# Moving the middle blocks as two partition halves, block by block: a softmax-gradient kernel on one Trainium2 core

## The chip, the core and the metric

The kernel runs on one core of one Trainium2 chip. The metric is the device time of one execution in microseconds (us). Three runs of the kernel before gave 1248.84, 1248.91 and 1249.3 us; the median is 1248.91 us.

## What is computed

The input is a float32 array of 8 x 1024 rows with 8192 logits each, and one integer label for each row. The output is the gradient of the cross-entropy loss: the softmax of each row, with 1 subtracted at the label.

```python
logits_max = np.max(logits, axis=-1, keepdims=True)
exp_logits = np.exp(logits - logits_max)
softmax = exp_logits / np.sum(exp_logits, axis=-1, keepdims=True)
...
one_hot[batch_idx, seq_idx, labels] = 1.0
return (softmax - one_hot).astype(np.float32)
```

Input and output are 268.4 MB each, and each is moved once.

## The kernel before

**Tiles.** The 8192 rows are cut into 32 blocks of 256 rows. In a block each of the 128 partitions holds G = 2 neighbouring rows (t0 and t1), 32 KB each, which lie one behind the other in device memory. A block is therefore 8.39 MB, and one partition's share of it is one run of 64 KB. On-chip the tile X has SLOTS = 3 places for a block, so block b + 3 goes where block b was. All work on a row is done in place in X.

**Work on one row t** (each "row" is 128 partitions x 8192):
- `row_max` (L141): VectorE (DVE) takes the negated maximum, a tensor_reduce.
- `exponentials` (L149): ScalarE (ACT) writes exp(x - max) over the row and sums it.
- `mark` (L157): two short ACT operations prepare the one-hot row as bytes in PSUM (`hot`), two rows ahead. It has to wait until the row that used this half of `hot` is finished.
- `finish` (L169): DVE takes the reciprocal of the sum and then does x * r - hot in one scalar_tensor_tensor. For the last two rows this is done in two halves of the columns.

**Transfers.** Three strings, one letter for each of the 32 blocks, say how a block moves and in which order it is worked. `PIECES` (L88) gives the pieces of a letter: "r" is two transfers, one for each row, over all 128 partitions in runs of 32 KB; "s" is four, each one row over every other partition (0, 2, 4, ... or 1, 3, 5, ...); "w" is one transfer over all 128 partitions in runs of 64 KB.
- `load(b)` (L101) issues the loads of block b on the SP queue (the odd partitions of "s" on the ACT queue). A piece waits for those stores of block b - 3 that touch the same partitions and rows (`meets`, L94).
- `store(t)` (L114) is called behind the finish of each row and issues on the ACT queue those pieces whose last row is t, after a wait for that finish. The last two rows are stored in two column halves each, on SP and ACT.
- Before: loads are "s" for blocks 0 to 2, "r" for 3 and 4, "w" for 5 to 28 and "r" for 29 to 31. All stores are "r".

**Order.** It is written out by hand in the loop at L244. Engines take their instructions strictly in the order in which this loop issues them. With the letter "r" in `ORDER`, DVE works a row ahead: max(t1), finish(t0), max of the next block's t0, finish(t1). The next block's first maximum therefore stands on DVE ahead of the finish of this block's second row. The store of t0 is issued between, right behind finish(t0). With the letter "b" (L247) DVE does max(t0), max(t1), finish(t0), finish(t1) and turns to the next block only then. Loads of block b + 3 are put on SP at the end of turn b in both orders.

All these operations go through the helper `run` (L71), so the profile gives them all line L76; they are told apart by their tiles and shapes.

Of the kernel before, what the change touches and what calls it, by code (L numbers as in the profile page):

```python
# [7 lines left out]
P = 128  # L8
G = 2
SLOTS = 3  # L10

LOADS = "sssrrwwwwwwwwwwwwwwwwwwwwwwwwrrr"
STORES = "rrrrrrrrrrrrrrrrrrrrrrrrrrrrrrrr"
ORDER = "rrrrrrrrrrrrrrrrrrrrrrrrrrrrrrrr"


@with_exitstack
def kernel(
# [45 lines left out]
    with tc.tile_critical():  # L64
# [6 lines left out]
        def run(engine, waits, counter, method, **operands):  # L71

            waits = list(dict.fromkeys(waits))
            for w in waits[:-1]:
                engine.wait_ge(*w)  # L75
            instruction = getattr(engine, method)(**operands)  # L76
            for w in waits[-1:]:
                instruction._wait_ge(*w)
            step = 16 if method == "dma_start" else 1
            instruction.then_inc(counter, step)  # L80
            count[counter.name] = count.get(counter.name, 0) + step
            return counter, count[counter.name]

        every, rows = slice(0, P), slice(0, G)
        one = [slice(j, j + 1) for j in range(G)]
        halves = [slice(i, P, 2) for i in range(2)]
        sides = [slice(i * V // 2, (i + 1) * V // 2) for i in range(2)]
        PIECES = {  # L88
            "r": [(every, js) for js in one],
            "s": [(ps, js) for js in one for ps in halves],  # L90
            "w": [(every, rows)],
        }

        def meets(a, b):  # L94
            sets = [[set(range(*d.indices(n))) for d, n in zip(p, (P, G))] for p in (a, b)]
            return all(x & y for x, y in zip(*sets))
# [4 lines left out]
        def load(b):  # L101
            loaded[b] = []
            before = stored.get(b - SLOTS, [])
            for q, piece in enumerate(PIECES[LOADS[b]]):
                ps, js = piece
                free = [w for other, w in before if meets(piece, other)]
                queue = nc.scalar if LOADS[b] == "s" and ps == halves[1] else nc.sync
                w = run(
# [5 lines left out]
        def store(t):  # L114
            b, j = divmod(t, G)
            stored.setdefault(b, [])
            if t >= T - G:
# [6 lines left out]
                return  # L124
            for q, piece in enumerate(PIECES[STORES[b]]):
                ps, js = piece
# [30 lines left out]
        def mark(t):  # L157
            if t >= T:
                return
            w = run(  # L160
                nc.scalar, ([made] if t < G else [freed[t - G]]) + ([marked[t - 1]] if t else []), act, "activation",
                out=away[:], in_=count16[:], func=Act.Abs, bias=at(word, t), scale=1.0,
            )
            marked[t] = run(
                nc.scalar, [w], act, "activation",
                out=hot[:, t % G, :], in_=away[:], func=Act.Relu, bias=at(unit, t), scale=at(minus, t),
            )
# [76 lines left out]
        for b in range(B):  # L244
            t0, t1 = b * G, b * G + 1
            nxt = t1 + 1
            if ORDER[b] == "b":  # L247
                if t0 not in maxed:
# [20 lines left out]
            mark(t0 + G)  # L269
            ahead = nxt < T and ORDER[b + 1] == "r"  # L270
            if ahead:
# [41 lines left out]
```

## Time and profile before

| what | value |
|---|---|
| median of 3 runs | 1248.91 us |
| span of the profiled execution (first to last instruction) | 1246.6 us |
| DVE busy | 1120.2 us, 90% |
| ACT busy | 722.7 us, 58% |
| moved by DMA | 536.98 MB, mean 431 GB/s |

The page's span is the time that it gives for its execution; the median of the runs is 2.3 us longer. In the profile "DMA" in a table by slices is the mean busy share of the core's 16 DMA engines, in tenths where it is one digit. A "packet" is one contiguous run, so 32 or 64 KB here, and a few bytes for the signal that a transfer has landed. q1 is the queue that SP issues on, q10 that of ACT. "us to landing" counts from the issue of a transfer to its last byte.

### The profile page before, as it was taken

To read this page: it belongs to the slowest core of one execution; us is meant where nothing else is said; L and a number is where in the kernel's file an instruction comes from. 1 tells how busy PE (TensorE), PEld (TensorE's weight loads), DVE (VectorE), ACT (ScalarE), POOL (GpSimd) and SP (SyncE) were. 2 spreads that over 40 slices of the span, in tenths; PEclk is the share of its full clock that TensorE was granted. 3 is DMA by queue.
4 is the path that set the end of the run, shared out by engine and by line. 5 is a ranking of instruction groups with operands and counts; after the bars stand their busy time and mean duration, and the time that the engine had idled before them with its cause. 6 is when DMAs were issued, how large, how long until landed. Compare 5 with 4: busy or idle time off the path is not lost.

```text
span 1246.6 us, 809 instructions
## 1 busy us (share of the span) xinstructions
PE 0.4 (0%) x2; PEld 0.3 (0%) x2; DVE 1120.2 (90%) x208; ACT 722.7 (58%) x257; POOL 2.3 (0%) x7
## 2 busy tenths in 40 slices
PE   0000000000000000000000000000000000000000
PEld 0000000000000000000000000000000000000000
DVE  5999998889988889888898888998889988899995
ACT  2866664556555565465655655556556555566662
POOL 0000000000000000000000000000000000000000
DMA  9999999999999999999999999999999999999998
GB/s 406 413 431 434 437 432 444 435 437 421 433 429 437 443 423 433 434 431 435 430 441 435 422 435 435 434 440 426 432 434 431 433 446 434 422 430 435 429 434 383
DMA packets 15413, 536.98 MB, mean 431 GB/s; under 512 B 1808, under 2 KB 1808, under 8 KB 1840
## 3 DMA queue, kind: packets, MB, share of 16 engines
q10 hardware_dynamic: 9744, 276.89, 51.5%
q1 hardware_dynamic: 5664, 260.05, 48.3%
q14 instruction: 5, 0.04, 0.0%
HBM read 268.50 MB, written 268.44 MB: 431 GB/s over the span
## 4 chain that ended last, share of the span: by engine, by line
DMA 59%; DVE 26%; issue 11%; ACT 3%; DVEq 0%; ACTq 0%; SPq 0%
DMA X<-in_logits_dram 33%; DMA out_dram<-X 26%; DVE X L76 15%; DVE m L76 10%; ACT X L76 2%; DVEq L64 0%; DVE r L76 0%; ACT hot L76 0%; ACT away L76 0%; ACTq L76 0%; DVEq L75 0%; ACTq L308 0%; SPq L64 0%
## 5 line engine op out<-in xcount | busy, mean ns | idle before, releaser
L76 ACT ACTIVATE X<-X,m 128x8192 f32<-128x8192 f32 x64 | 455.8, 7122 | 365.2 <-DVE m L76 365.2
L76 DVE TENSOR_REDUCE m<-X 128x1 f32<-128x8192 f32 x64 | 555.6, 8682 | 105.4 <-DMA X<-in_logits_dram 105.4
L76 DVE SCALAR_TENSOR_TENSOR X<-X,r,hot 128x8192 f32<-128x8192 f32 (+1 forms) x66 | 560.1, 8489 | 3.8 <-ACT hot L76 1.6
L76 ACT ACTIVATE away<-count,word 128x2048 bf16<-128x2048 int16 x64 | 128.1, 2001 | 127.0 <-DVE X L76 127.0
L76 ACT ACTIVATE hot<-away,unit,minus 128x2048 int32<-128x2048 bf16 x64 | 131.9, 2061 | 2.1
L76 ACT ACTIVATION_READ_ACCUMULATOR X<-X,m 128x1 f32 x64 | 11.9, 186 | 0.0
L76 DVE RECIPROCAL r<-s 128x1 f32<-128x1 f32 x64 | 9.8, 153 | 0.0
L76 ACT ACT_TABLE_LOAD x1 | 1.3, 1283 | 5.3 <-issue 5.3
L76 DVE CAST lab_f<-lab_raw 32x256 f32<-32x256 int32 x1 | 0.5, 536 | 2.7 <-DMA lab_raw<-in_labels_dram 2.7
L76 POOL IOTA count<- 128x2048 int16 x1 | 1.8, 1823 | 0.0
L76 DVE TENSOR_TENSOR unit<-unit,part 128x64 f32<-128x64 f32 x3 | 0.7, 225 | 0.1
L76 DVE CAST lab<-hot 128x64 int32<-128x64 f32 x1 | 0.2, 224 | 0.5 <-PE hot L76 0.5
L76 DVE TENSOR_SCALAR part<-minus 128x64 f32<-128x64 f32 x3 | 0.6, 194 | 0.1
L76 PE MATMUL hot<-ident,lab_f 32*128 32x32 f32 x2 | 0.4, 298 | 3.3 <-DVE lab_f L76 3.3
L76 PEld LDWEIGHTS hot<-ident,lab_f 32*128 32x128 f32 x2 | 0.3, 192 | 3.3 <-DVE lab_f L76 3.3
L76 DVE CAST minus<-lab 128x64 f32<-128x64 int32 x1 | 0.2, 195 | 0.0
L76 DVE TENSOR_SCALAR word<-part 128x64 f32<-128x64 int32 x1 | 0.2, 195 | 0.0
L76 DVE TENSOR_SCALAR lab<-lab 128x64 int32<-128x64 int32 x1 | 0.2, 195 | 0.0
L76 DVE TENSOR_SCALAR unit<-minus 128x64 f32<-128x64 f32 x1 | 0.2, 195 | 0.0
L76 DVE TENSOR_SCALAR part<-lab 128x64 int32<-128x64 int32 x1 | 0.2, 194 | 0.0
L76 DVE TENSOR_SCALAR minus<-unit 128x64 f32<-128x64 f32 x1 | 0.2, 194 | 0.0
L76 POOL TENSOR_SCALAR_AFFINE_SELECT ident<-ident 32x32 f32<-32x32 f32 x1 | 0.2, 203 | 0.1
(5 smaller groups left out, 0.5 us busy)
## 6 DMA issues: line engine op xcount, KB each, us to landing
out_dram<-X ACTq DMA_DIRECT2D x62, 4096.0 KB, 30.4
X<-in_logits_dram SPq DMA_DIRECT2D x10, 4096.0 KB, 28.1
X<-in_logits_dram SPq DMA_DIRECT2D x6, 2048.0 KB, 32.6
X<-in_logits_dram ACTq DMA_DIRECT2D x6, 2048.0 KB, 37.1
out_dram<-X SPq DMA_DIRECT2D x2, 2048.0 KB, 12.7
out_dram<-X ACTq DMA_DIRECT2D x2, 2048.0 KB, 11.9
X<-in_logits_dram SPq DMA_DIRECT2D x24, 33.4
lab_raw<-in_labels_dram ACTq DMA_DIRECT2D x1, 64.0 KB, 1.8
```

The source lines that it names most:

```text
L76: instruction = getattr(engine, method)(**operands)
```

## The change

```diff
-LOADS = "sssrrwwwwwwwwwwwwwwwwwwwwwwwwrrr"
-STORES = "rrrrrrrrrrrrrrrrrrrrrrrrrrrrrrrr"
-ORDER = "rrrrrrrrrrrrrrrrrrrrrrrrrrrrrrrr"
+LOADS = "sssrrccccccccccccccccccccccccrrr"
+STORES = "rrccccccccccccccccccccccccrrrrrr"
+ORDER = "bbbbbbbbbbbbbbbbbbbbbbbbbbbbbbbb"
...
+        blocks_p = [slice(i * P // 2, (i + 1) * P // 2) for i in range(2)]
...
             "w": [(every, rows)],
+            "c": [(ps, rows) for ps in blocks_p],
```

The new letter "c" is two transfers, one for partitions 0 to 63 and one for partitions 64 to 127, each with both rows: 64 runs of 64 KB, 4.19 MB. Loads of blocks 5 to 28 are "c" where they were "w", and stores of blocks 2 to 25 are "c" where they were "r". As block b + 3 follows block b in its place, each lower half is loaded behind the store of the same lower half, and each upper half behind that of the upper. A "c" store covers both rows, so both of its transfers are issued behind finish(t1), where "r" issued the first behind finish(t0). All blocks are worked in the order "b". The first and last blocks move as before.

## The prediction

> **What bounds the kernel now.** I read the page's first lines, then DMA by stretches of time, then the chain that ended last. On the page:
>
> ```profile
> span 1246.6 us, 809 instructions
> PE 0.4 (0%) x2; PEld 0.3 (0%) x2; DVE 1120.2 (90%) x208; ACT 722.7 (58%) x257; POOL 2.3 (0%) x7
> DMA  9999999999999999999999999999999999999998
> DMA packets 15413, 536.98 MB, mean 431 GB/s; under 512 B 1808, under 2 KB 1808, under 8 KB 1840
> q10 hardware_dynamic: 9744, 276.89, 51.5%
> q1 hardware_dynamic: 5664, 260.05, 48.3%
> ```
>
> The two queues fill 99.8% of the time of 16 DMA engines: 0.998 x 1246.6 = 1244.1 us of work, and 2.5 us without. The table by stretches (us, engines, clock, DMA share, GB/s in the last column) says where:
>
> ```profile
> 2.00:44.00 42.00, 0.41 (x2) 0.28 (x2) 28.84 (x18) 20.71 (x8) 1.13 (x1) 1.00 1.00 426
> 44.00:166.00 122.00, 0.00 (x0) 0.00 (x0) 121.75 (x22) 81.77 (x30) 0.00 (x0) 1.00 1.00 430
> 166.00:1093.00 927.00, 0.00 (x0) 0.00 (x0) 829.86 (x144) 534.11 (x190) 0.00 (x0) 1.00 1.00 433
> 1093.00:1215.00 122.00, 0.00 (x0) 0.00 (x0) 121.75 (x21) 78.94 (x28) 0.00 (x0) 1.00 1.00 433
> 1215.00:1246.60 31.60, 0.00 (x0) 0.00 (x0) 18.02 (x7) 7.21 (x2) 0.00 (x0) 1.00 0.89 382
> ```
>
> DMA is full from 2 us to the tail, with the same 426 to 433 GB/s when only loads run (before 44 us) and when both directions do. DVE waits in the middle (830 of 927 us). So time is bytes over rate; an edit can gain only idle DMA, and there are 2.5 us of it.
>
> Per engine, q1 gives 0.483 x 16 x 1246.6 / 260.05 = 37.05 us per MB, q10 0.515 x 16 x 1246.6 / 276.89 = 37.10. That is 27 GB/s an engine, and 2.43 us for a run of 64 KB. q1 holds most of the 64 KB runs and q10 nearly all the 32 KB ones: the length of a run is worth 0.05 us per MB, under 1 us in all.
>
> How the engines share the work is seen in the middle of the trace, the DMA of 20 us in slices of 0.5 us (bytes are counted where a packet starts):
>
> ```profile
> DMA  9900193990009499300799960099300794960049
> GB/s 1704 393 0 0 66 852 131 918 1180 0 0 0 852 197 524 1442 131 0 0 328 721 393 1442 262 0 0 393 1573 131 0 0 328 655 197 1704 262 0 0 197 786
> q1 hardware_dynamic: 96, 6.29, 72.5%
> q10 hardware_dynamic: 95, 2.59, 30.0%
> ```
>
> Packets start in waves: peaks at slices 1, 9, 16, 23, 28 and 35, mostly 3.5 us apart, which is one 64 KB load (2.43 us) and one 32 KB store (1.21 us). All sixteen engines take a load together, then a store together, spread over about 0.75 us. This decides below.
>
> The chain repeats every two blocks:
>
> ```profile
> 482.00 26.58 DMA out_dram<-X
> 508.59 33.63 DMA X<-in_logits_dram
> 542.25 0.04 DVE m L76
> ...
> 551.04 8.76 DVE X L76
> 559.82 26.10 DMA out_dram<-X
> ```
>
> 77.8 us for two blocks, 38.9 each, is their 33.55 MB at 431 GB/s. The chain is stretched to the DMA rate; it does not set it.
>
> **The change part by part.**
>
> *Order "b" and the later store.* The DVE and ACT instructions are the same ones:
>
> ```profile
> L76 DVE TENSOR_REDUCE m<-X 128x1 f32<-128x8192 f32 x64 | 555.6, 8682 | 105.4 <-DMA X<-in_logits_dram 105.4
> L76 DVE SCALAR_TENSOR_TENSOR X<-X,r,hot 128x8192 f32<-128x8192 f32 x62 | 542.4, 8748 | 3.7 <-ACT hot L76 1.6
> L76 ACT ACTIVATE X<-X,m 128x8192 f32<-128x8192 f32 x64 | 455.8, 7122 | 365.2 <-DVE m L76 365.2
> ```
>
> A block costs DVE 2 x 8.68 + 2 x 8.75 + 2 x 0.15 (reciprocal) = 35.2 us in either order. In "b" the exponentials of t1 (7.1 us) end before finish(t0) (8.75 us) does, so finish(t1) waits for nothing. From the trace in order of time:
>
> ```profile
> 482.00 0.34 ACTq L76 DMA_DIRECT2D out_dram<-X  x1
> 499.44 0.34 ACTq L76 DMA_DIRECT2D out_dram<-X  x1
> 499.89 2.00 ACT L76 ACTIVATE away<-count,word 128x2048 bf16<-128x2048 int16 x1 [2.08 <-DVE X L76]
> 501.92 2.06 ACT L76 ACTIVATE hot<-away,unit,minus 128x2048 int32<-128x2048 bf16 x1
> 508.59 77.68 SPq L76 DMA_DIRECT2D X<-in_logits_dram  x3
> ```
>
> ACT now waits in one place for finish(t1) before it issues both store halves; behind it stand one mark and the next block's first exponentials, which need a maximum 8.7 us later anyway, and a mark takes 4.1 us (2.00 + 2.06). The first row's store, which now goes out 17.4 us ahead of the second's, waits for it.
>
> Does DMA run dry for it? With both queues equally served, a block's store takes 38.7 us (twice 8.39 MB at 433 GB/s); the lower half of block b + 3 loads behind the lower half of the store, the upper half needs 19.4 us more, then DVE 35.2: 93.3 us of the three periods (116.2 us) that a place in X has. 23 us are left, and two of the three places always hold a transfer. Cost 0. If that cover fails, DMA stands idle between a block's finish and its store's successors, priced with the rivals.
>
> *Transfers.* 24 loads become 48; stores stay at 66 issues. An issue takes 0.34 us on ACT; SP issues three in 77.7 us. More than 4,000 extra packets on q10 cost nothing visible above, so 24 x 16 more signals cost under 0.1 us. Cost 0.
>
> *64 KB stores, half the partitions.* Run length: between -1 us and 0. The partition range is what matters, and no transfer before stays within 64 neighbouring partitions. The bounds:
>
> ```profile
> X<-in_logits_dram SPq DMA_DIRECT2D x6, 2048.0 KB, 32.6
> X<-in_logits_dram ACTq DMA_DIRECT2D x6, 2048.0 KB, 37.1
> ```
>
> *Lower bound, nothing:* these "s" loads also have 64 partitions each, and they are all that moves until 44 us, at 426 GB/s. So 64 partitions as such are not slow. But they are every other one, spread over the whole memory.
>
> *Upper bound, twice the time:* at full rate each engine moves 27 GB/s with sixteenths of all the partitions, loads alone no faster than loads and stores. If the way into a group of partitions carries what one engine brings, sixteen engines inside one half have eight ways, two engines on each. Because they run in waves, the two meet: a packet takes 4.86 us instead of 2.43 less the offset between the two. Across a wave 0.75 us wide two engines are some 0.25 us apart, a tenth of a packet: factor 1.9, for loads and for stores, since each wave is of one direction. A lower half in flight beside an upper half does not help, for all engines serve one piece, then the other.
>
> The "s" row is nearest in size, the waves nearest in kind; no row decides. I take factor 1.9, and keep 1 and 2 for the range.
>
> The Trainium skill speaks against this change: its page "SBUF — State Buffer", section "Door 1: The DMA port swizzle", says that partitions 0 to 63 reach only the eight even ports of sixteen and 64 to 127 only the odd ones, at about 218 GB/s. Every other partition reaches all sixteen by that table, so the "s" rate agrees with it; no run here yet shows a contiguous half. By its figure the 402.65 MB of "c" would take an estimated 1847 us. The page "DMA: Bandwidth & Descriptors", section "Rules for kernel authors", says two transfers to disjoint partition halves "serialize".
>
> *Sum.* "c" carries 24 loads and 24 stores of 8.39 MB: 402.65 of 536.98 MB, 75.0%, so 932.9 of the 1244.1 us of DMA work; the rest is 311.2 us. 932.9 x 1.9 = 1772.5; with 311.2 and 2.5 idle the span is 2086 us. The runs' median is 2.3 us above the profiled span: **2089 us**. DVE's 35.2 us a block lie inside some 74 us of DMA.
>
> **The rivals.**
>
> *A, no change:* the halves run at full rate (each engine can reach any partition at 27 GB/s, or each half keeps to its own eight engines and both run side by side). For it: the "s" loads. No row speaks against it. DMA stays full, 1244.1 + 2.5 + 2.3 = 1249 us, 1247 to 1251; not slower. It decides if a 64 KB packet into a half still takes 2.43 us. By the page of the Trainium skill named above it would not.
>
> *B, half of it:* only one direction is limited, or the two engines of a way fall out of step and one loads while the other stores. Factor 1.5: 1399.4 + 311.2 + 4.8 = 1715 us. For it: an engine that takes its packet from the other queue first stays out of step. Against it: the waves are still sharp at 322 us.
>
> *C, four engines on one way:* if the 64 partitions are dealt so that sixteen engines first crowd into 32, factor up to 4: 3731.6 + 316.0 = 4048 us. Nothing in the rows excludes it.
>
> *D, DMA runs dry a little:* full rate, but in the tail the last block's 35.2 us of DVE come after its load, and if the backlog of stores has by then drained, up to half of that (17.6 us) is idle: 1249 to 1267. Against it: 20 us of queued stores and 8.4 MB of the block before (19.4 us) cover it.
>
> *E, faster:* at most 2.5 us of idle and 1 us of run length, 1245 us.
>
> **How the numbers follow.** Forecast (both directions limited, factor about 1.75 to 2, 1950 to 2182 us) 0.47; B, with factors of 1.1 to 1.75, 0.17; C 0.08; A 0.16; D 0.09; E 0.03. The range must reach from A to the full factor 2 (1865.8 + 316.0 = 2182): 1246 to 2190 holds 0.89; leaving A out would lose too much together with C. The forecast's own range is 1950 to 2190. About 0.2% (2.5 us) is what a measurement can tell from no change. Faster 0.03 (E); same 0.17 (A and a little of D); slower 0.80.
>
> **What would show it.** Right: in the middle the page's DMA digits stay 9 while GB/s falls from 433 to about 228; time of q1 and q10 per MB rises from 37 us an engine to about 62 (three quarters at 1.9); DVE's share falls near 54% with long waits of the maximum for loads; the first 60 us are as before. GB/s near 290 in the middle means B, 433 means A, near 110 means C. DMA digits under 9 with full packets mean D. I am wrong if the half-memory transfers keep 433 GB/s; then the limit sits in the engines, not in the way to the partitions.

## The result and the profile after

The change makes the kernel slower: 1653.42 us median of four runs (1644.65 to 1696.59), against 1248.88 us for the kernel before beside it. The ratio is 1.322, 95% interval [1.319, 1.325]; the longest run, 3% above the shortest, is left out of it. The profiled execution has a span of 1653.2 us. Its page:

```profile
span 1653.2 us, 857 instructions
PE 0.4 (0%) x2; PEld 0.3 (0%) x2; DVE 1120.5 (68%) x208; ACT 722.7 (44%) x257; POOL 2.3 (0%) x7
DMA  9999999999999999999999999999999999999997
GB/s 408 420 436 339 321 336 328 314 309 309 311 304 316 300 304 301 316 303 321 293 309 298 301 300 297 292 303 297 298 293 301 290 293 303 291 333 431 435 432 307
q1 hardware_dynamic: 6048, 260.05, 57.2%
q10 hardware_dynamic: 6672, 276.89, 42.1%
```

DMA is as full as before, and the compute engines do the same work in the same time. The rate falls where the first half-memory transfer starts, in the fourth slice (124 to 165 us), and is back when the last is done. So the time did not go into waiting for an issue or into an order; the same bytes go more slowly. The stretch from 200 to 1400 us, at 305 GB/s (queue, packets, megabytes, share of 16 engines' time), says in which direction:

```profile
q1 hardware_dynamic: 3492, 183.44, 61.5%
q10 hardware_dynamic: 3476, 182.59, 38.6%
```

Loads (q1) now take 0.615 x 16 x 1200 / 183.44 = 64.4 us per MB and engine, where they took 37.05: factor 1.74. Stores (q10) take 40.6 instead of 37.10: factor 1.09. For the 201.3 MB that "c" carries each way this is 201.3 x 27.35 / 16 = 344 us for loads and 201.3 x 3.5 / 16 = 44 us for stores, 388 of the 407 us by which the span grew. Idle DMA has grown as well, from 2.5 us to 11.6 us (0.7% of the span); some 10 us are left. This splits the time that packets took; the runs below ask what each part costs by itself.

The waves are gone too. The DMA of 20 us in the middle of the changed kernel, in slices of 0.5 us:

```profile
DMA  6509996666999389956939399090935796939699
GB/s 262 131 0 393 393 393 262 262 262 262 655 655 393 131 262 262 393 131 262 524 131 524 131 393 524 0 786 0 524 131 131 262 524 262 393 131 524 262 524 393
```

In the 20 us of the kernel before that the prediction shows, nearly all packets began in peaks of up to 1704 GB/s with empty slices between. Here hardly a slice is empty: some engines load while others store. The start and length of each packet in the trace say the same: in these 20 us never fewer than two and never more than eleven of the sixteen engines are storing.

DVE only waits longer for loads (the group's idle time in the last columns was 105.4 us):

```profile
L76 DVE TENSOR_REDUCE m<-X 128x1 f32<-128x8192 f32 x64 | 553.2, 8680 | 504.3 <-DMA X<-in_logits_dram 504.3
```

### The profile page after: what moved, and what is told of

Read it like the earlier page. It is cut to its first block, busy times and chain, and to the rows that moved or that the text cites. A ratio compares the mean times of both kernels' runs of the same rounds, so it can differ in the third digit from the quotient of the medians.

```text
span 1653.2 us, 857 instructions
## 1 busy us (share of the span) xinstructions
PE 0.4 (0%) x2; PEld 0.3 (0%) x2; DVE 1120.5 (68%) x208; ACT 722.7 (44%) x257; POOL 2.3 (0%) x7
## 4 chain that ended last, share of the span: by engine, by line
another core or an unknown queue 43%; DVE 24%; DMA 16%; issue 15%; ACT 1%; DVEq 0%; SPq 0%; ACTq 0%
DVE X L76 12%; DVE m L76 11%; DMA X<-in_logits_dram 8%; DMA out_dram<-X 7%; ACT X L76 1%; DVE r L76 0%; DVEq L64 0%; ACT hot L76 0%; ACT away L76 0%; SPq L76 0%; ACTq L76 0%; DVEq L75 0%; ACTq L310 0%; ACTq L75 0%
```

## Experiments

My theory after the result (W): what is written into 64 neighbouring partitions has half of the ways, and reading out of them is hardly limited. Rivals: the order and the late store (O), limited reading that something hides (S), and the mere cutting into two transfers of 64 runs (H).

### Each part alone

Loads in halves, all stores by rows:

```diff
-STORES = "rrccccccccccccccccccccccccrrrrrr"
+STORES = "rrrrrrrrrrrrrrrrrrrrrrrrrrrrrrrr"
```

> Only the loads of blocks 5 to 28 go as two contiguous halves; all stores are by rows as before, order b. Theory W (what is written into 64 neighbouring partitions has half of the ways; a load packet took 64.4 us per MB and engine instead of 37.05, a store packet 40.6 instead of 37.1): 201.3 MB x 27.35 / 16 = 344 us more, about 1593 us; if the waves of the kernel before stay in step, factor 1.9 and 1668 us. Rival O (the order and the late store of both rows are the cost): about 1249 us, since the stores are not late here. Rival S (stores out of partition halves are as limited, and only their being out of step hides it): some 1450 to 1600 us.

Measured: 1675.45 us, ratio 1.342 [1.336, 1.348], slower than with the stores in halves as well. From 200 to 1000 us:

```profile
q1 hardware_dynamic: 2275, 118.69, 61.8%
q10 hardware_dynamic: 4246, 123.80, 37.9%
```

Loads take 0.618 x 16 x 800 / 118.69 = 66.6 us per MB, factor 1.80. That is close to the 1668 us that theory W gave for waves in step, and above rival S's 1450 to 1600. The order is not the cost: stores leave early here.

Stores in halves, loads of whole blocks:

```diff
-LOADS = "sssrrccccccccccccccccccccccccrrr"
+LOADS = "sssrrwwwwwwwwwwwwwwwwwwwwwwwwrrr"
```

> Only the stores of blocks 2 to 25 go as two contiguous halves; loads are whole blocks as before, order b. Theory W: stores cost 201.3 MB x 3.5 / 16 = 44 us more, 1250 to 1293 us. Rival O (order and late store): near 1650 us, as both are here. Rival S (reading out of a half is limited as writing is): with waves back in step up to factor 1.9, 1668 us.

Measured: 1525.12 us, ratio 1.221 [1.217, 1.225], and from 200 to 1000 us:

```profile
q10 hardware_dynamic: 2594, 136.25, 53.9%
q1 hardware_dynamic: 2338, 136.45, 44.5%
```

Stores take 50.6 us per MB, factor 1.36, and the loads of whole blocks beside them 0.445 x 16 x 800 / 136.45 = 41.7, factor 1.13. Theory W falls in its second half: reading out of a half is limited too, and rival S is right that the combination hides it. Alone the two parts cost 427 and 277 us; together they cost 405. Of the 277 us some 43 come with 64 KB stores beside 64 KB loads even without halves ("Smaller costs" below), so that the halves of the stores are worth some 234.

The order alone, all transfers as before:

```diff
-LOADS = "sssrrccccccccccccccccccccccccrrr"
-STORES = "rrccccccccccccccccccccccccrrrrrr"
+LOADS = "sssrrwwwwwwwwwwwwwwwwwwwwwwwwrrr"
+STORES = "rrrrrrrrrrrrrrrrrrrrrrrrrrrrrrrr"
```

> Order b for all blocks, all transfers as in the kernel before. Theory W: DMA stays full, 1247 to 1252 us. Rival O: well above 1260 us, with DMA digits under 9.

Measured: 1248.60 us, ratio 0.9999 [0.999, 1.0009]. Rival O is out.

The whole change with other halves:

```diff
-        blocks_p = [slice(i * P // 2, (i + 1) * P // 2) for i in range(2)]
+        blocks_p = halves
```

> The whole change, but the two halves are every other partition (0, 2, 4, ... and 1, 3, 5, ...) instead of neighbouring ones; numbers, sizes, queues, waits and order of the transfers are the same. Theory W: all ways are reached, 1247 to 1255 us. Rival H (two transfers of 64 runs each are slower whatever their partitions, by their count or by how sixteen engines share 64 runs): near 1653 us.

Measured: 1256.70 us, ratio 1.0067 [1.0035, 1.0100], just above theory W's 1247 to 1255. From 200 to 1000 us:

```profile
q1 hardware_dynamic: 3297, 173.08, 50.4%
q10 hardware_dynamic: 3298, 172.43, 49.8%
```

That is 37.3 us per MB for loads and 37.0 for stores, the rate of the kernel before. Number, size, queues, waits and order of the transfers are those of the change; only which partitions stand in a transfer differs, and with it 397 of 405 us are gone. Rival H is out.

### The disputed cost by itself

A kernel of nothing but transfers in 19 stages. It leaves out the softmax. Like the other kernels of transfers alone, it was executed once. Its core:

```python
for pieces in (WHOLE, HALVES, EVERY2, QUARTERS, EVERY4, EIGHTHS):
    loads(pieces)
loads(HALVES, (sp, act))
for pieces in (WHOLE, HALVES, EVERY2, QUARTERS, EVERY4, EIGHTHS):
    stores(pieces)
stores(HALVES, (act, sp))
for lps, sps in ((WHOLE[0], WHOLE[0]), (lo, lo), (lo, hi), (lo, WHOLE[0]), (WHOLE[0], lo)):
    ...
```

> No softmax at all: only transfers, in stages, each stage waiting for the one before to have landed. Seven stages load three blocks (25.2 MB), seven store three blocks, five do both. Pieces: whole blocks over 128 partitions; halves (0 to 63, 64 to 127); every other partition; quarters of 32 neighbours; every fourth partition; eighths of 16 neighbours; halves with the lower on one queue and the upper on the other at once. Then load beside store: whole and whole (33.6 MB); lower half and lower half (16.8 MB); lower and upper (16.8 MB); load lower half beside store whole; load whole beside store lower half (25.2 MB each). Theory W2 (eight ways a half, each carrying one engine's 27 GB/s, for writes and for reads alike): whole, every other and every fourth about 60 us a stage; halves and quarters about 116 us in both directions; eighths about 232 us (four ways). Lower and upper half at once: 116 us if the engines keep in step, down to 60 if they fall out of it. Rival W (writes alone are limited): stores of halves 60 us. Rival S2 (one limit for reads and writes of a half together): lower beside lower 77 us and lower beside upper 39 to 77 us; with separate ways for reads and writes these two are alike. Rival H (64 runs are dealt badly): every other partition is slow too.

Some of its stages in the table by stretches (us, POOL, clock, DMA share, GB/s). Loads: whole, halves, every other partition, quarters, eighths, lower and upper half from two queues. Stores: whole, halves, eighths, two queues. Then load beside store: whole and whole, lower and lower, lower and upper.

```profile
2.00:61.10 59.10, 0.00 (x0) 1.00 0.98 419
62.80:185.20 122.40, 0.00 (x0) 1.00 1.00 206
187.20:246.40 59.20, 0.00 (x0) 1.00 0.99 424
247.80:370.00 122.20, 0.00 (x0) 1.00 0.99 203
432.40:657.40 225.00, 0.00 (x0) 1.00 1.00 112
660.10:779.10 119.00, 0.00 (x0) 1.00 1.00 211
780.90:839.20 58.30, 0.00 (x0) 1.00 0.99 429
840.80:958.70 117.90, 0.00 (x0) 1.00 0.97 211
1198.80:1315.20 116.40, 0.00 (x0) 1.00 0.86 214
1316.80:1403.30 86.50, 0.00 (x0) 1.00 0.94 286
1404.60:1504.10 99.50, 0.00 (x0) 1.00 0.91 337
1506.00:1564.30 58.30, 0.00 (x0) 1.00 0.96 287
1566.20:1625.20 59.00, 0.00 (x0) 1.00 0.96 285
```

Alone, halves run at half the rate in both directions: 206 for 419 to 424 GB/s, and 211 for 429. All sixteen engines are busy meanwhile (share 0.97 to 1.00), so the engines do not stand idle; they are held up. Lower beside lower and lower beside upper are alike, so loads and stores do not share a way with each other, and rival S2 is out. Sending the lower and the upper half from two queues at once gains 2% for loads and 36% for stores. The Trainium skill, page "SBUF — State Buffer", section "Can I just issue two DMAs to hit both halves?", says that this gains 6%; the loads, with 2%, bear it out, the stores here do not.

The eighths looked odd: 112 GB/s for loads but 214 for stores. I formed theory P from it (writes limited by groups of partitions, reads only by the half as a whole) and tested it with stores that never leave sixteen, and never leave eight, partitions:

```python
for ps in (slice(0, 16), slice(0, 8)):
    phase([(sp, True, s, 3, ps) for s in range(SLOTS)])
    phase([(act, False, s, b, ps) for b in range(8) for s in range(1)])
...
mixed(WHOLE, WHOLE)
mixed(WHOLE, EVERY2)
mixed(EVERY2, EVERY2)
...
```

> Transfers alone again, without softmax. First small sets of partitions: loads of partitions 0 to 15 (3 MB), eight stores of the same partitions 0 to 15 (8.4 MB, always the same sixteen, so that engines out of step cannot mix groups), then the same with partitions 0 to 7 (1.6 and 4.2 MB), then sixteen stores in turn from 0 to 15 and 64 to 79 (16.8 MB). Theory P (writes are limited by groups of partitions, reads only by half of the memory as a whole, some 215 GB/s): loads 112 and 56 GB/s, stores 215 GB/s for sixteen and about 200 for eight partitions. Theory W2 (both by groups): stores 112 and 56 GB/s. Then load beside store, two blocks each way, 64 KB runs unless said: whole and whole (337 GB/s in the run before); whole and every other partition; every other and every other; load every other, store whole; load whole, store by rows of 32 KB; both by rows; halves and halves; load halves, store whole; load whole, store halves; whole and whole again. Theory T (64 KB runs in both directions over 128 partitions disturb each other): whole and whole 330 to 350, by rows 425 to 433, every other and every other 425 to 433. Theory F (337 was left over from the stages before it): whole and whole 425 to 433 here. Halves and halves: 285 to 300 by the run before.

Loads and stores of 0 to 15, loads and stores of 0 to 7:

```profile
62.50:91.20 28.70, 0.00 (x0) 1.00 0.96 107
93.30:175.40 82.10, 0.00 (x0) 1.00 0.99 102
176.60:205.00 28.40, 0.00 (x0) 1.00 0.48 55
206.80:288.80 82.00, 0.00 (x0) 1.00 0.50 51
```

Theory P falls: both directions have about a quarter of the full rate for sixteen partitions and an eighth for eight. The 214 of the stored eighths is probably what engines reach that are out of step and so stand in different eighths (DMA share 0.86 there). One stage speaks for it: sixteen stores in turn from partitions 0 to 15 and 64 to 79 took 103 us for 16.8 MB, 163 GB/s instead of 102. Why the loaded eighths keep in step is open.

The stages of load beside store show in small what the whole kernels did. With the loads in halves, stores in halves and stores of whole blocks; then loads of whole blocks with stores in halves:

```profile
910.70:1023.70 113.00, 0.00 (x0) 1.00 0.96 295
1025.30:1142.90 117.60, 0.00 (x0) 1.00 0.95 284
1145.00:1245.20 100.20, 0.00 (x0) 1.00 0.95 333
```

Beside loads in halves, stores in halves are no slower than stores of whole blocks: 113.0 against 117.6 us for the same bytes.

Which partitions share a way was asked with two at a time:

```python
for d in (1, 2, 3, 4, 8, 12, 16, 20, 24, 28, 32, 36, 40, 44, 48, 52, 56, 60, 64, 68, 96, 100):
    phase([(act, False, 0, b, slice(0, d + 1, d)) for b in range(4)])
```

> Transfers alone, without softmax. Each stage stores two partitions, 0 and d, four times (64 KB a partition), d from 1 to 100; two engines carry it, one partition each. If 0 and d share a way, a packet takes about 5.1 us as in the small sets before, else 2.42 us. Then loads of such pairs, and stores of every 32nd, 16th and 8th partition, of every 4th below 64 and of every 2nd below 32. Theory G (groups of four neighbours, repeated every 32 partitions below 64, the upper half with ways of its own): 5.1 us for d of 1, 2, 3 and 32, 2.42 us for all other d, 64 and 96 among them. Theory G2 (the groups are shifted above 32, so that every whole transfer in step meets no clash though each engine has eight neighbours in a row): 2.42 us for 32 and 5.1 us for another d between 36 and 60. This also tells whether an engine in a whole transfer can clash with another one once they are out of step, for which whole beside whole at 341 GB/s speaks.

Each stage stores the same 0.52 MB; the rows (from one pause to the next) are for d of 3, 4 and 32:

```profile
106.20:128.30 22.10, 0.00 (x0) 1.00 0.12 24
128.30:139.80 11.50, 0.00 (x0) 1.00 0.11 46
207.50:229.50 22.00, 0.00 (x0) 1.00 0.12 24
```

20.5 us of transfer for d of 1, 2, 3 and 32, and 9.7 to 10.5 us for all eighteen others. Loads were tried with six of these pairs: 15 us for d of 1 and 32, 8 to 9 us for 4, 36, 64 and 96. Theory G holds: groups of four neighbours, repeated after 32, and other ways for the upper half. This is the table of the Trainium skill, page "SBUF — State Buffer", section "Door 1: The DMA port swizzle", and here it agrees in every pair tried. All pairs contain partition 0; that the other groups are alike is taken from the rates above (halves and quarters 206 and 203, sixteen partitions 107, eight 55 GB/s). A half of neighbours therefore reaches eight ways with sixteen engines, and every other partition reaches sixteen.

### Why the stores were hidden

Two engines at a time, eight loads and eight stores each, on one way ("near") or on two ("apart"):

```python
beside(NEAR, NEAR)
beside(NEAR, UPPER)
beside(NEAR, APART)
beside(APART, NEAR)
beside(APART, APART)
```

> Transfers alone, two engines at a time (two partitions a transfer, runs of 64 KB): each engine has eight loads on one queue and eight stores on the other. Near pairs lie on one way (neighbours in one group of four), apart pairs on two. In order, and then once more: loads near, stores near on the same way; loads near, stores near on the way of the upper half; loads near, stores apart; loads apart, stores near; both apart. Alone, a near packet took 5.1 us and an apart packet 2.43 us. Fair model (two engines on a way halve each other only while both are on it in one direction, each direction has its own way): near and near from 9.7 us for a load with a store when in step down to 4.9 when out of step, loads and stores lengthened alike; loads near, stores apart 2.4 + up to 5.1. Rival R (a store's reading goes on behind a load that is held up in writing): loads 4 to 5 us, stores 2.4 to 3 us with near and near, and hardly longer than with stores apart; loads apart, stores near shows little over 2.43 for loads. Both apart: 4.9 us a pair of packets; if more, the engine itself holds up two directions. Then whole transfers of 64 KB runs with both queues at once: two loads; four stores; a load and a store of the like block; of another block. If two loads and four stores run at 425 to 433 GB/s and a load beside a store at 340, the loss is in mixing directions, not in using two queues.

Near and near (54.9 us), then loads apart with stores near (48.2 us), then both apart (44.0 us):

```profile
q1 hardware_dynamic: 32, 1.05, 6.9%
q10 hardware_dynamic: 32, 1.05, 5.5%
```

```profile
q10 hardware_dynamic: 32, 1.05, 6.9%
q1 hardware_dynamic: 32, 1.05, 5.5%
```

```profile
q1 hardware_dynamic: 32, 1.05, 6.2%
q10 hardware_dynamic: 32, 1.05, 6.1%
```

A share times 16 times the stretch, over 16 packets, is the mean packet. Near and near: loads 0.069 x 54.9 = 3.8 us, stores 3.0 us; when the stage came a second time, 3.6 and 3.4. Loads near, stores apart: loads 3.8, stores 2.5 us. Loads apart, stores near: loads 2.7, stores 3.3 us. Both apart: 2.7 us each. Alone, near packets took 5.1 us. How near and near works shows in 10 us of it, in slices of 0.25 us, where each 262 is the start of one packet:

```profile
GB/s 262 0 262 0 0 0 0 0 0 0 262 0 262 0 0 0 0 0 0 0 0 0 0 0 0 0 262 0 0 0 262 0 0 0 0 0 262 0 0 262
q1 hardware_dynamic: 8, 0.26, 10.0%
q10 hardware_dynamic: 8, 0.26, 6.5%
```

Both engines start a store (slices 1 and 3), both a load 2.5 us later (11 and 13), both a store 4 us later (27 and 31), and both a load 2.5 us later (37 and 40). They are in step, both storing from the same way at the same time, and yet a store takes 0.065 x 16 x 10 / 4 = 2.6 us, while a load takes 4.0. This speaks against the fair model, in which two stores at once must hold each other up as they do alone. It is what rival R expects: while an engine is held up in writing its load, the reading for its next store already goes on.

The load need not be held up for that. In the stage with loads apart and stores near, from 233.2 to 238.5 us, both engines load and then both store from one way, in step:

```profile
q1 hardware_dynamic: 4, 0.13, 6.8%
q10 hardware_dynamic: 4, 0.13, 5.7%
```

Each row counts two packets of data. The loads take 0.068 x 16 x 5.3 / 2 = 2.9 us and the stores 2.4; the four stores just before, which have no load ahead of them, take 5.1 each. Nor is it always the stores that go free. Later in near and near, from 94.5 to 100.5 us, the engines are out of step, one loading while the other stores:

```profile
q10 hardware_dynamic: 4, 0.13, 10.4%
q1 hardware_dynamic: 4, 0.13, 5.1%
```

Here the two loads take 2.4 us and the two stores 5.0 on average. That the engine reads ahead is argued from these times; no row shows its reading and writing apart. Why with sixteen engines it is the loads that pay, in the changed kernel as in the stages alone, stays open.

The last test asks it of the whole kernel: loads in neighbouring halves, stores as every other partition, which by themselves reach all ways.

```diff
-STORES = "rrccccccccccccccccccccccccrrrrrr"
+STORES = "rraaaaaaaaaaaaaaaaaaaaaaaarrrrrr"
...
+            "a": [(ps, rows) for ps in halves],
```

> Loads of the change (halves of neighbouring partitions), but its stores leave as every other partition, which alone reach all ways; order b, runs of 64 KB both ways. Theory R (beside loads that are held up, a store from a half is hardly held up itself, so the halves of the stores add nothing to those of the loads): 1620 to 1690 us, about as the change itself (1653) and as loads in halves alone (1675). Fair model (both directions lengthen alike and each is paid): some 150 us or more under the change, near 1500 us.

Measured: 1697.37 us median, four runs from 1666.62 to 1699.53; they spread too much for an interval. That is about theory R's 1620 to 1690 us and far from the fair model's 1500. Even the shortest run is longer than the change's median of 1653 us, so setting the stores free of the halves gains nothing. From 200 to 1000 us of the profiled run (1695.96 us) stores take 38.5 us per MB, where the change has 41.0 in the same stretch, but loads 69.4 where it has 62.5: what the stores no longer lose, the loads take on. A gain of some us could still hide here, for loads and stores are cut in different ways in this run, and that has a price of its own ("Smaller costs").

### Smaller costs

Runs of 64 KB in both directions, without any halves:

```diff
-LOADS = "sssrrccccccccccccccccccccccccrrr"
-STORES = "rrccccccccccccccccccccccccrrrrrr"
+LOADS = "sssrrwwwwwwwwwwwwwwwwwwwwwwwwrrr"
+STORES = "rrwwwwwwwwwwwwwwwwwwwwwwwwrrrrrr"
```

> Loads of blocks 5 to 28 and stores of blocks 2 to 25 each as one whole transfer over all 128 partitions in runs of 64 KB; order b; no partition halves. Theory W2 or P (only what stays in half of the partitions is limited): 1247 to 1260 us. Theory T (64 KB runs both ways disturb each other at 337 instead of 433 GB/s): 402.65 MB cost 265 us more, up to 1515 us, less where the engines stay in step.

Measured: 1290.83 us (two runs), ratio 1.034 [1.024, 1.044]. Theory T has the direction, but 43 of its 265 us. In the stages alone, whole beside whole gave 343 GB/s, every other beside every other 416, and loads of 64 KB beside stores of 32 KB 423:

```profile
394.40:492.30 97.90, 0.00 (x0) 1.00 0.93 343
579.90:660.60 80.70, 0.00 (x0) 1.00 0.99 416
748.80:828.20 79.40, 0.00 (x0) 1.00 0.99 423
```

Two whole loads from two queues ran at 412 GB/s and four whole stores at 432, so the loss comes with the mixing of directions. Why 64 KB beside 64 KB loses and 64 beside 32 KB does not stays open.

Every other partition for one direction alone (the same edit of `blocks_p`, with the stores, or the loads, of the kernel before):

> Every other partition as in the run before, but for the loads alone; stores by rows, order b. The run with both gave 1256.7 us, 8 us more, most of it idle DMA at the very end (7.4 us idle after 1240 us against 3.5). Theory D (stores of whole blocks leave late and leave DMA idle in the tail): 1247 to 1251 us here. Rival (two load transfers instead of one cost it, by more and shorter pieces): 1254 to 1260 us.

Measured: 1252.85 us, ratio 1.0034 [1.0022, 1.0046], between the two ranges.

> Every other partition for the stores alone; loads of whole blocks, order b. Theory D: 1253 to 1260 us, with DMA idle in the tail. Rival (the load transfers cost it): 1247 to 1251 us.

Measured: 1307.07 us, ratio 1.048 [1.045, 1.051]. Neither range holds it. Theory D does not explain this: from 200 to 1000 us the rate is 409 GB/s, and the tail is not idle. It is again 64 KB loads of whole blocks beside 64 KB stores, and as open as the run above. The last 50 us of the order alone, of every other partition both ways, and of the stores alone:

```profile
1196.40:1246.40 50.00, 0.00 (x0) 0.00 (x0) 28.86 (x8) 14.43 (x4) 0.00 (x0) 1.00 0.94 403
```

```profile
1204.90:1254.90 50.00, 0.00 (x0) 0.00 (x0) 28.90 (x8) 14.43 (x4) 0.00 (x0) 1.00 0.85 364
```

```profile
1252.60:1302.60 50.00, 0.00 (x0) 0.00 (x0) 30.10 (x8) 14.43 (x4) 0.00 (x0) 1.00 0.94 405
```

With every other partition both ways DMA is busy 0.85 instead of 0.94 of it, which is 4.5 us more idle of the 8. Theory D puts that down to the late stores, but with late stores alone the tail is as full as with the order alone (0.94), and with the loads alone nearly so (0.93). What empties it when both go in two pieces is open.

None of these beats the kernel before, whose DMA is idle for 2.5 us in all.

## Why the prediction was wrong, point by point

- **The bound.** Right: DMA stayed full, 11.6 us of 1653 idle, and the time grew because the rate fell.
- **Order "b" at 0.** Right: ratio 0.9999.
- **24 more transfers at 0.** Nearly: two loads of every other partition for one whole load cost 4.3 us (1.0034); I had put the number of transfers under 0.1 us.
- **64 KB stores, -1 to 0 us.** Wrong in sign: with whole blocks and nothing else changed but the order, ratio 1.034, some 43 us; with both directions as every other partition, the nearest to the change, 8 us. The row that I used compared run lengths on separate queues, not both ways at once.
- **Two engines on each way.** Right, and shown: halves alone run at 206 and 211 GB/s, pairs on one way take 5.1 us a packet where 4.86 was worked out, and every other partition is free of it.
- **"Factor 1.9, for loads and for stores, since each wave is of one direction."** This step failed. It put 420 us on the loads and 420 on the stores (0.9 of 933 us in all). Loads cost 344 us (factor 1.74; 1.80 with the stores by rows), stores 44 (factor 1.09). The loads' term was a fifth too large, the stores' term more than nine times. The runs of single parts say it more sharply: the loads' halves alone cost 427 us, the 420 of the sum, and the stores' halves, 277 us by themselves, add nothing to them (405 together). So the step that failed is to price both directions as if each ran alone and to add the prices. Two things were seen in its place. The waves did not last once packets were held up; even in the kernel before, from 300 to 1000 us, none or all of the sixteen engines are storing in only about half of the time, less sharply than in the 20 us that I took. And two stores that meet on a way, each behind a load, can take 2.4 to 2.6 us in step, against 5.1 without a load ahead. How much each of the two contributes stays open.
- **The rivals.** B had the time, 1715 us for factor 1.5, and named the pattern (one direction limited) as one of its two ways. Its reason is half right: both directions are limited alone, one is hidden in company. C is out: groups of four crowd only when a transfer stays within fewer than 32 partitions. A is out. D is small: the changed kernel's DMA is busy 0.79 of its last 53 us, some 11 us idle, but its reason is not shown, since late stores alone leave no idle tail.

## What to carry to other kernels

When DMA is the bound, ask of every transfer which partitions it touches together, not only how many or how long its runs are: 64 neighbours ran at half the rate and 64 alternating ones at the full rate. The limit that halved each direction alone cost factors of 1.74 and 1.09 when both ran, so try each part of a two-way change by itself, and both together, before adding their prices. Full DMA digits do not mean full rate (here 305 GB/s at a share of 1.00); time per megabyte of each queue tells which direction pays.

## What the runs showed of the hardware that was not expected

- Partitions 0 and 32 share a way, 0 and 4 or 0 and 64 do not: 20.5 against 9.7 us for the same bytes.
- Two engines on one way take 5.1 us for 64 KB each when both only store, but 2.4 to 2.6 us when each stores behind a load, whether that load took 2.9 or 4.0 us.
- Two engines on ways of their own, each with loads and stores in turn, take 2.7 us a packet instead of 2.43; sixteen of them, over whole blocks, fall to 343 GB/s. The cause is open.
